# A two-layer decoder trunk handed its inputs in the layouts that its engines read: feature rows for the activations, 4 KB rows for the weights

## The chip, the cores and the metric

The kernel runs on one core of a Trainium2 chip, as one launch. The metric is device microseconds (us) of that launch; the median of three runs is taken. The work of the host ahead of the launch and behind it (which the change adds to) is not part of the metric.

## The reference

Two layers over 512 tokens with 2048 features, float32. Layer 0 is sparse attention: an indexer scores the causal keys, each query keeps 128 of them, and softmax attention with rotary positions runs over these. Layer 1 is stick-breaking attention over keys and values made from layer 0's output. Each layer ends alike:

```
y = (o * silu(g)) @ w_out                 # o: attention, g: gate path
x = layer_norm(4**0.25 * x + y, ln_g[i], ln_b[i])
x = x + (p[i] @ w_ple[i]) * sigmoid(x @ w_ple_gate[i])
```

The inputs are `x` (512 x 2048, tokens in rows), `p` (2 x 512 x 256), positions, the weights (each with the input features in rows) and the LayerNorm rows; the output has tokens in rows.

## The kernel before

All activations are kept with features on the 128 partitions and the 512 tokens along the free dimension, as tiles of 128 x 512 (`tt`, 78 buffers), 16 tiles to a full activation. float32 products are made of three matmuls (`mm3`): both operands are split into a high part, rounded by ScalarE, and the rest, taken by VectorE (`split` for activations, lines 103 and 104; `split_w` for weights, lines 314 and 315).

The kernel is one list of chunks, written out by hand in the order in which TensorE (PE) takes them. A chunk is 512 KB of weights (128 x 1024), loaded by `load` on SP's queue six chunks ahead into one of six `raw` buffers, split two chunks ahead, and used by 24 matmuls of 512 columns (lines 119 to 121). `run` emits them; small work (attention of a head, stores) is hung on the chunks by `after`, `mid`, `defer` and `soon`, and so takes its place in the order of each engine. Instructions of one engine run in the order of the program.

The stages, with their place in the span:

- start, 0 to 8 us: `prologue` loads x and the first weights, runs transposes on a constant to warm PE (`warm`), and turns and splits the first two x tiles.
- the value block, 8 to 58 us: `natural_block`, eight chunks. The weights are the moving operand; in the middle of each of seven chunks (`mid`) the next two x tiles are turned on PE by `transpose_x` (line 464) and split.
- the indexer, keys, queries and gates of layer 0 with the attention of its 16 heads, to 650 us. `ln_columns` (line 456) turns the LayerNorm rows there.
- `mix_out(0)`, `ple_chunks(0)`, `gate_block(0)`: output projection, embedding, LayerNorm and gate, to 1010 us. `prep_p` (line 778) turns the embeddings. `out_done` adds x back, from the high and the low part of its split (lines 802 and 803), which are therefore kept until then. Behind it come the sums of LayerNorm.
- layer 1's values, and from 1052 us on `quads`: keys, queries, values and gates by Strassen's scheme, with half-sized matmuls of 256 columns (line 198). Some chunks are sums of weight blocks: 60 of them come by a DMA that adds, issued by POOL (`add_load`, line 300), 60 by VectorE (line 305).
- `mix_out(1)`, `ple_chunks(1)`, `gate_block(1)`, from 1745 us to the end. `x1_load` (line 949) brings back layer 0's output, which was put into DRAM. `out_store` turns each output tile by four transposes (line 1117), copies it by ScalarE (line 1118) and stores it (line 1119); the last tile goes in two halves.

Weights lie in DRAM as the caller gives them, so a chunk is gathered in pieces of 512 B (128 columns), 1 KB (256) or 2 KB (512), in layer 0's query and gate blocks by two DMAs.

Of the kernel before, what the change touches and what calls it, by code (L numbers as in the profile page):

```python
# [74 lines left out]
class Kernel:  # L75
# [66 lines left out]
    def block(self, view, cols, xs, done, pops=1, col=0):  # L142
        outs = [Out(KT, lambda ps, i=i: done(i, ps), col) for i in range(2)]
        self.chunks += [self.chunk4(view, cols, kc, outs, xs, pops=pops) for kc in range(KT // 4)]
# [5 lines left out]
    def chunk4(self, view, cols, kc, outs, xs, pre=None, pops=1):  # L150
        nc = self.nc

        def loads(raw):
            r = raw.rearrange("p (k c) -> p k c", k=4)
            if view is None:
                cols(raw, kc)
            elif cols[1] == cols[0] + P:
                nc.sync.dma_start(r, view[:, 4 * kc:4 * kc + 4, cols[0]:cols[0] + 2 * P])
            else:
# [7 lines left out]
    def natural_block(self, view, col, xs, done):  # L167
        outs = [Out(KT, lambda ps, t=t: done(t, ps)) for t in range(NT)]
        for kc in range(KT // 2):
            def loads(raw, kc=kc):  # L170
                r = raw.rearrange("p (k c) -> p k c", k=2)
                for k in ((0, 1), (1, 2)) if kc == 0 else ((0, 2),):
                    self.nc.sync.dma_start(r[:, k[0]:k[1], :], view[:, 2 * kc + k[0]:2 * kc + k[1], col:col + T])
# [4 lines left out]
            ch = Chunk(loads, mms)  # L178
            ch.parts = 2 if kc == 0 else 1
            self.chunks.append(ch)  # L180

    def natural_halves(self, view, col, x, done):
        outs = [Out(KT, lambda ps, t=t: done(t, ps)) for t in range(NT)]
        for kc in range(KT // 2):
            def loads(raw, kc=kc):
                self.nc.sync.dma_start(raw.rearrange("p (k c) -> p k c", k=2),
                                       view[:, 2 * kc:2 * kc + 2, col:col + T])

            mms = [((k * T, 0), outs[t], (lambda m=2 * kc + k, t=t: x(m, t))) for t in range(NT) for k in range(2)]
            self.chunks.append(Chunk(loads, mms))  # L190
# [10 lines left out]
    def quads(self, sources, forms, done):  # L201
# [4 lines left out]
        def product(q, name, form, acc, start, stop, after, fresh=None, add=None, grown=None, plus=None):  # L206
# [7 lines left out]
            def rows(half, block):  # L214
                view, c = block
                return view[:, half::2, c:c + P]

            def loads(raw):
                nc.sync.dma_start(raw.rearrange("p (k c) -> p k c", k=8), rows(*fresh))

            ch = Chunk(loads if fresh else None, [])
# [74 lines left out]
    def add_load(self, c):  # L296
# [3 lines left out]
        self.nc.gpsimd.dma_start(ch.raw.rearrange("p (k c) -> p k c", k=8), ch.add, accum_op=OP.add)  # L300
# [88 lines left out]
def body(tc, x, p, positions, w_in_a, w_out_a, w_q_b, w_kv_b, w_out_b, ln_g, ln_b, w_ple, w_ple_gate, freq, out):  # L389
    nc = tc.nc  # L390
    with tc.tile_pool(name="const", bufs=1) as const, \
# [7 lines left out]
        _emit(k, x[0], p, positions, w_in_a[0], w_out_a[0], w_q_b[0], w_kv_b, w_out_b[0], ln_g, ln_b, w_ple,  # L399
              w_ple_gate, freq, out[0])  # L400


def _emit(k, x, p, positions, w_in, w_out_a, w_q, w_kv, w_out_b, ln_g, ln_b, w_ple, w_gate, freq, out):
    nc, const = k.nc, k.const
    kview = lambda w: w.rearrange("(k p) c -> p k c", p=P)
    win_v, wq_v, wkv_v = kview(w_in), kview(w_q), kview(w_kv)
    wout_v = [kview(w_out_a), kview(w_out_b)]
    wgate_v = [kview(w_gate[i]) for i in range(2)]
    wple_v = [kview(w_ple[i]) for i in range(2)]
# [8 lines left out]
    lnrow = const.tile([64, P], F32, name="lnrow")  # L418

    def load_small():  # L420
        nc.sync.dma_start(fr, freq)
        nc.sync.dma_start(pos_i, positions.to_broadcast([P, T]))
        nc.sync.dma_start(lnrow[0:32, :], ln_g.rearrange("i (m c) -> (i m) c", c=P))
        nc.sync.dma_start(lnrow[32:64, :], ln_b.rearrange("i (m c) -> (i m) c", c=P))

    xv = x.rearrange("(t p) d -> p t d", p=P)
# [21 lines left out]
    lncol = const.tile([P, 64], F32, name="lncol")  # L448
# [5 lines left out]
    def ln_columns():  # L454
        ps = k.ps("s")
        nc.tensor.transpose(ps[:, 0:64], lnrow, ident[0:64, 0:64])
        nc.vector.tensor_copy(lncol, ps[:, 0:64])

    def transpose_x(m):
        b, c = divmod(m, 2)  # L460
        ps = k.ps("s")
        for t in range(NT):
            off = (t % 2) * 2 * P + c * P
            nc.tensor.transpose(ps[:, t * P:(t + 1) * P], xin[b][t // 2][:, off:off + P], ident)  # L464
        xT[m] = k.split(ps)
        if c == 1:
            xin[b] = None
# [73 lines left out]
    def ki_block():  # L541
        o = Out(KT, lambda ps: ki_done(0, ps))
        for kc in range(2):
            def loads(raw, kc=kc):
                r = raw.rearrange("p (k c) -> p k c", k=8)
                nc.sync.dma_start(r[:, :, 0:64], win_v[:, 8 * kc:8 * kc + 8, KI0:KI0 + 64])
                nc.sync.dma_start(r[:, :, 64:128], win_v[:, 8 * kc:8 * kc + 8, WI0:WI0 + 64])

            mms = [(P * j, o, (lambda m=8 * kc + j: xT[m])) for j in range(8)]
            k.chunks.append(Chunk(loads, mms))  # L550
# [169 lines left out]
    def first_x(ms):  # L720
        for m in ms:
            transpose_x(m)

    k.natural_block(win_v, V0, xs, lambda t, ps: v_done(va, t, ps))
    for n in range(7):
        k.chunks[n].mid = lambda n=n: first_x(range(2 * n + 2, 2 * n + 4))
# [5 lines left out]
    def prologue():  # L732
        early = LOAD_LEAD - HL_BUFS + 1
        for n in range(early):
            load_x(n)
            k.ahead(n - LOAD_LEAD)
        for n in range(early, 8):
            load_x(n)
        load_small()
        warm(8)  # L740
        first_x(range(2))
        warm(8)
# [7 lines left out]
    for m in range(0, 8, 2):  # L750
        k.block(win_v, (I0 + m * P, I0 + (m + 1) * P), xs, lambda i, ps, m=m: qi_done(m + i, ps), col=P)
    k.chunks[16].after = lambda: st["later"].pop(0)()
    k.chunks[12].after = ln_columns
    for g in range(0, KV_A, 2):
        k.block(win_v, (K0 + g * P, K0 + (g + 1) * P), xs, lambda i, ps, g=g: k_done(g + i, ps))
    for h in range(HEADS):
        k.block(win_v, (Q0 + h * P, G0 + h * P), xs, lambda i, ps, h=h: q_done_a(h, i, ps))
# [6 lines left out]
    def load_p(layer):  # L764
        pb.clear()
        pv = p[layer][0].rearrange("(t p) d -> p t d", p=P)
        for t in range(0, NT, 2):
            pt = k.tt(s="pin")
            nc.sync.dma_start(pt.rearrange("p (t d) -> p t d", t=2), pv[:, t:t + 2, :])
            pb.append(pt)  # L770

    def prep_p(layer):
        pT[layer] = []
        for f in range(2):
            ps = k.ps("s")
            for t in range(NT):
# [381 lines left out]
```

## Time and profile before

| | |
|---|---|
| median of 3 runs | 2142.22 us (2141.61 to 2142.41) |
| the profiled execution | 2142.52 us |
| its span in the trace | 2140.6 us |
| matmul instructions (transposes among them) | 12305 |
| of these transposes of x, p, the output and the LayerNorm rows | 64, 16, 64, 1 |
| read from and written to DRAM | 234.65 MB, 12.06 MB |

The profile shows one execution. Engines are PE (matmul), PEld (its weight loads, which overlap), DVE (VectorE), ACT (ScalarE), POOL (GpSimd) and SP (which issues most DMAs). A duration is that of one instruction from start to end; matmuls overlap, so the distance of two starts is shorter than a duration. L119 is line 119 of the kernel.

### The profile page before, as it was taken

How to read it: one execution, taken by the hardware profiler on the slowest of the kernel's cores; microseconds unless marked ns; L12 is line 12 of the kernel's file. 1: busy time of each engine (PE TensorE's matmuls, PEld its weight loads, DVE VectorE, ACT ScalarE, POOL GpSimd, SP SyncE). 2: the span in 40 equal slices, each digit the busy share in tenths (PEclk: the TensorE clock that was granted, in tenths of full speed). 3: DMA queues.
4: the chain of work that ended last, by engine and by line, in shares of the span. 5: the costliest groups of instructions: out<-in, count | busy, mean ns of one | idle time of the engine just before them, and what ended most of it. 6: DMA issues, size and time to landing. Idle time of an engine off the chain costs nothing.

```text
span 2140.6 us, 31013 instructions
## 1 busy us (share of the span) xinstructions
PE 2120.4 (99%) x12305; PEld 1876.6 (88%) x12305; DVE 1354.5 (63%) x2065; ACT 967.8 (45%) x1530; POOL 262.1 (12%) x287
## 2 busy tenths in 40 slices
PE   9999999999999999999999999999999999999999
PEld 8987888888888887888899999999999988887887
DVE  4576976566566547635778777777777765447432
ACT  3564345455453226423555555445555453226422
POOL 5111000000000100000022122112222111010000
PEclk9999999999999999999999999999999999999999
DMA  7332332222222232433567777777867863332331
GB/s 222 109 89 80 106 90 79 70 79 69 79 89 92 93 101 79 131 115 121 116 135 133 150 141 138 149 148 146 160 124 146 167 200 109 118 118 78 100 120 57
DMA packets 368816, 248.72 MB, mean 116 GB/s; under 512 B 13664, under 2 KB 354720, under 8 KB 368672
## 3 DMA queue, kind: packets, MB, share of 16 engines
q1 hardware_dynamic: 306272, 215.29, 34.9%
q0 software_dynamic: 62400, 31.46, 11.9%
q8 instruction: 96, 1.57, 0.3%
q14 instruction: 48, 0.39, 0.1%
HBM read 234.65 MB, written 12.06 MB: 115 GB/s over the span
## 4 chain that ended last, share of the span: by engine, by line
PE 91%; DVE 4%; issue 3%; ACT 2%; POOL 1%; DMA 0%; SPq 0%; POOLq 0%; DVEq 0%; ACTq 0%
PE g L198 25%; PE g L119 19%; PE g L120 19%; PE g L121 19%; PE s L627 2%; PE o L120 1%; PE o L121 1%; PE o L119 1%; PE s L119 1%; DVE wl L315 1%; PE s L120 1%; PE s L121 1%; DVE z L888 1%; PE s L561 1%; DVE z L887 1%
## 5 line engine op out<-in xcount | busy, mean ns | idle before, releaser
L315 DVE TENSOR_TENSOR wl<-raw,wh 128x1024 fp32r<-128x1024 f32 (+1 forms) x453 | 555.6, 1231 | 388.0 <-ACT wh L314 384.3
L119 PE MATMUL g<-h,wh 128*128 128x512 f32 (+1 forms) x1808 | 704.6, 390 | 3.3 <-ACT h L103 3.3
L120 PE MATMUL g<-l,wh 128*128 128x512 f32 (+1 forms) x1808 | 698.8, 387 | 3.6 <-DVE l L104 3.6
L121 PE MATMUL g<-h,wl 128*128 128x512 f32 (+1 forms) x1808 | 698.6, 386 | 0.5 <-DVE wl L315 0.5
L314 ACT CAST wh<-raw 128x1024 fp32r<-128x1024 f32 (+1 forms) x453 | 473.2, 1049 | 330.9 <-PE g L120 216.3
L198 PE MATMUL g<-f,wh 128*128 128x256 f32 x3360 | 619.4, 284 | 0.0
L198 PEld LDWEIGHTS g<-f,wh 128*128 128x128 f32 x3360 | 528.6, 192 | 0.8
L198 PE MATMUL g<-f,wl 128*128 128x256 f32 x1680 | 475.5, 283 | 1.9 <-DVE wl L315 1.9
L119 PEld LDWEIGHTS g<-h,wh 128*128 128x128 f32 x1808 | 340.3, 188 | 74.4 <-ACT h L103 5.4
L120 PEld LDWEIGHTS g<-l,wh 128*128 128x128 f32 x1808 | 340.2, 188 | 70.3 <-DVE l L104 5.9
L121 PEld LDWEIGHTS g<-h,wl 128*128 128x128 f32 x1808 | 340.0, 188 | 67.0 <-DVE wl L315 1.0
L198 PEld LDWEIGHTS g<-f,wl 128*128 128x128 f32 x1680 | 322.0, 192 | 3.5 <-DVE wl L315 2.7
L300 POOL DMA_DIRECT2D raw<-in_w_q_b_dram x60 | 94.4, 1894 | 571.9 <-issue 244.1
L104 DVE TENSOR_TENSOR l<-s,h 128x512 fp32r<-128x512 f32 (+1 forms) x128 | 72.9, 617 | 45.7 <-ACT h L103 45.7
L504 POOL TENSOR_TENSOR rb<-rb,sin 128x512 f32<-128x512 f32 (+2 forms) x29 | 36.0, 1240 | 475.7 <-ACT rb L502 320.6
L685 ACT ACTIVATE pr<-pr,s 128x128 f32<-128x128 f32 (+1 forms) x64 | 36.0, 563 | 126.1 <-DVE s L684 125.7
L103 ACT CAST h<-s 128x512 fp32r<-128x512 f32 (+1 forms) x128 | 61.1, 540 | 59.9 <-PE s L464 31.0
L837 POOL TENSOR_TENSOR a<-a,sq 128x512 f32<-128x512 f32 x30 | 40.3, 1343 | 338.9 <-ACT sq L835 338.7
L305 DVE TENSOR_TENSOR raw<-raw,raw 128x1024 f32<-128x1024 f32 x60 | 73.1, 1218 | 0.0
L700 DVE TENSOR_TENSOR_SCAN r<-keep,zeros 128x127 f32<-128x127 f32 (+1 forms) x64 | 54.3, 849 | 13.7 <-POOL keep L697 13.7
L505 DVE TENSOR_TENSOR ra<-ra,cos 128x512 f32<-128x512 f32 (+2 forms) x29 | 32.8, 1130 | 37.7 <-ACT ra L503 37.6
L835 ACT ACTIVATE sq<-z 128x512 f32<-128x512 f32 x30 | 19.0, 634 | 81.7 <-DVE z L828 81.7
(187 smaller groups left out, 1960.3 us busy)
## 6 DMA issues: line engine op xcount, KB each, us to landing
raw<-in_w_in_a_dram SPq DMA_DIRECT2D x134, 256.0 KB, 3.3
raw<-in_w_ple_gate_dram SPq DMA_DIRECT2D x64, 512.0 KB, 3.8
raw<-in_w_kv_b_dram SPq DMA_DIRECT2D x64, 512.0 KB, 6.4
raw<-in_w_q_b_dram SPq DMA_DIRECT2D x64, 512.0 KB, 6.9
raw<-in_w_q_b_dram POOLq DMA_DIRECT2D x60, 512.0 KB, 10.0
raw<-in_w_out_a_dram SPq DMA_DIRECT2D x32, 512.0 KB, 3.6
raw<-in_w_out_b_dram SPq DMA_DIRECT2D x32, 512.0 KB, 3.5
raw<-in_w_in_a_dram SPq DMA_DIRECT2D x31, 512.0 KB, 3.8
```

What stands on the lines that cost most here:

```text
L103: nc.scalar.copy(h[:, lo:w], src[:, lo:w])
L104: nc.vector.tensor_tensor(l[:, lo:w], src[:, lo:w], h.bitcast(F32)[:, lo:w], op=OP.subtract)
L119: nc.tensor.matmul(out, ah, bh, start=start, stop=False)
L120: nc.tensor.matmul(out, ah, bl, start=False, stop=False)
L121: nc.tensor.matmul(out, al, bh, start=False, stop=stop)
L198: nc.tensor.matmul(ps[:, :HALF], a, b, start=start and j == 0 and n == 0, stop=stop and j == KT // 2 - 1 and n == 2, skip_group_check=True)
L300: self.nc.gpsimd.dma_start(ch.raw.rearrange("p (k c) -> p k c", k=8), ch.add, accum_op=OP.add)
L305: self.nc.vector.tensor_tensor(ch.raw, ch.raw, ch.plus.raw, op=OP.add)
L314: nc.scalar.copy(ch.h[:, i:i + w], ch.raw[:, i:i + w])
L315: nc.vector.tensor_tensor(ch.l[:, i:i + w], ch.raw[:, i:i + w], ch.h.bitcast(F32)[:, i:i + w], op=OP.subtract)
L627: nc.tensor.transpose(banks[b][:, off + (i - j) * P:off + (i - j + 1) * P], a["p"][i][:, j * P:(j + 1) * P], ident)
L700: nc.vector.tensor_tensor_scan(r[:, 0:n - 1][:, ::-1], keep[:, 1:n][:, ::-1], zeros.to_broadcast([P, n - 1]), 1.0, op0=OP.mult, op1=OP.add)
```

## The change

The host hands over other arrays, and the kernel drops what turned them:

- `x`, `p` and the output have features in rows, the LayerNorm rows come as columns (128 x 64). `transpose_x`, `ln_columns` and the transposes of `prep_p` and `out_store` go, as does the copy in `out_store`. A tile of x or p is loaded in pieces of 2 KB and split from SBUF instead of PSUM.
- every weight chunk lies in DRAM as 128 rows of 4 KB, in the order of use; one DMA loads it (`whole`). Columns of the value weights of layer 1's first heads are held twice (`w_v` and `w_kv`).
- in the start, the order of the loads is x tile 0, half of the first weight chunk, x tile 1, the other half; the warm-up's 16 transposes stand in one group.
- layer 0's output projection loads x again (16 tiles on SP's queue) instead of keeping its split; the split is given up at the end of the last head. `out_done` has one addition.
- an output store is hung on the next chunk by `soon` instead of `defer_by`.

```
-    def chunk4(self, view, cols, kc, outs, xs, pre=None, pops=1):
-        def loads(raw):
-            r = raw.rearrange("p (k c) -> p k c", k=4)
...
-                for i in range(2):
-                    nc.sync.dma_start(r[:, :, i * P:(i + 1) * P], view[:, 4 * kc:4 * kc + 4, cols[i]:cols[i] + P])
+    def whole(self, src, n):
+        return lambda raw: self.nc.sync.dma_start(raw, src[n])
+    def chunk4(self, src, n, kc, outs, xs, pre=None, pops=1):
...
-        return Chunk(loads, mms, pre=pre, pops=pops)
+        return Chunk(self.whole(src, n), mms, pre=pre, pops=pops)
...
-        self.nc.gpsimd.dma_start(ch.raw.rearrange("p (k c) -> p k c", k=8), ch.add, accum_op=OP.add)
+        self.nc.gpsimd.dma_start(ch.raw, ch.add, accum_op=OP.add)
...
-    def load_x(b):
-        xin[b] = [k.tt(s="xin") for _ in range(2)]
-        for t in range(2):
-            nc.sync.dma_start(xin[b][t].rearrange("p (t c) -> p t c", t=2),
-                              xv[:, 2 * t:2 * t + 2, b * 2 * P:(b + 1) * 2 * P])
+    def load_x(m):
+        xin[m] = k.tt(s="xin")
+        nc.sync.dma_start(xin[m], xt[m])
...
-    def transpose_x(m):
-        b, c = divmod(m, 2)
-        ps = k.ps("s")
-        for t in range(NT):
-            off = (t % 2) * 2 * P + c * P
-            nc.tensor.transpose(ps[:, t * P:(t + 1) * P], xin[b][t // 2][:, off:off + P], ident)
-        xT[m] = k.split(ps)
+    def split_x(m):
+        xT[m] = k.split(xin.pop(m))
...
+    def first_loads(raw):
+        for i in range(2):
+            if i:
+                load_x(1)
+            nc.sync.dma_start(raw[:, i * T:(i + 1) * T], w_in[0][:, i * T:(i + 1) * T])
...
+    for kc in range(4):
+        k.chunks[kc - 4].then(lambda kc=kc: x_drop(kc))
...
     def prep_p(layer):
-        for f in range(2):
-            ps = k.ps("s")
-            for t in range(NT):
-                off = (t % 2) * 256 + f * P
-                nc.tensor.transpose(ps[:, t * P:(t + 1) * P], pb[t // 2][:, off:off + P], ident)
-            pT[layer].append(k.split(ps))
+        pT[layer] = [k.split(t) for t in pb]
...
-            nc.vector.scalar_tensor_tensor(z, xh.bitcast(F32), ALPHA, ps, op0=OP.mult, op1=OP.add)
-            nc.vector.scalar_tensor_tensor(z, xl.bitcast(F32), ALPHA, z, op0=OP.mult, op1=OP.add)
+        nc.vector.scalar_tensor_tensor(z, x1.pop(m), ALPHA, ps, op0=OP.mult, op1=OP.add)
...
-            if layer == 1 and kc == 1:
+            if kc == 1:
+                ch.then(lambda b=b: [x1_load(layer, 2 * b + i) for i in range(2)])
+    def x1_load(layer, m):
         x1[m] = k.tt(s="x1")
-        nc.sync.dma_start(x1[m], xd[m])
+        nc.sync.dma_start(x1[m], xd[m] if layer else xt[m])
...
     def out_store(m, v):
-        o = k.tt(s="out")
         for c in halves(m):
...
-                nc.tensor.transpose(ps[:, t * P:(t + 1) * P], v[:, t * P:(t + 1) * P], ident)
-            nc.scalar.copy(o[:, c], ps[:, c])
-            nc.sync.dma_start(outv[:, t0:t1, m * P:(m + 1) * P], o[:, c].rearrange("p (t c) -> p t c", t=t1 - t0))
+            nc.sync.dma_start(out[m, :, c], v[:, c])
```

## Rows read from the trace of the kernel before

**Rows 1.** The page, busy time, share and instructions of each engine.

```profile
PE 2120.4 (99%) x12305; PEld 1876.6 (88%) x12305; DVE 1354.5 (63%) x2065; ACT 967.8 (45%) x1530; POOL 262.1 (12%) x287
```

**Rows 2.** Stretches: length, busy PE, PEld, DVE, ACT, POOL, granted clock, DMA share, GB/s.

```profile
0.00:5.00 5.00, 2.67 (x11) 1.87 (x11) 0.23 (x2) 1.28 (x1) 1.28 (x9) 1.00 0.58 168
...
12.00:20.00 8.00, 8.00 (x45) 6.80 (x44) 3.63 (x5) 2.92 (x5) 0.00 (x0) 1.00 1.09 357
20.00:56.00 36.00, 36.00 (x180) 30.23 (x179) 16.19 (x19) 12.89 (x19) 31.36 (x23) 1.00 0.59 163
...
800.00:870.00 70.00, 66.31 (x282) 52.25 (x281) 55.96 (x78) 43.40 (x64) 2.59 (x2) 1.00 0.24 76
...
1095.00:1240.00 145.00, 143.10 (x1161) 141.29 (x1160) 110.67 (x152) 75.99 (x124) 30.96 (x45) 1.00 0.72 139
1240.00:1735.00 495.00, 495.00 (x4059) 492.08 (x4058) 362.63 (x473) 251.53 (x402) 102.03 (x128) 1.00 0.78 153
...
1770.00:1920.00 150.00, 150.00 (x667) 124.24 (x666) 69.33 (x76) 42.38 (x51) 17.58 (x13) 1.00 0.36 116
...
1920.00:1990.00 70.00, 66.76 (x281) 53.36 (x280) 55.52 (x77) 44.16 (x64) 2.58 (x2) 0.98 0.23 75
```

**Rows 3.** Order of time, PE, one chunk of the value block: start, length.

```profile
43.56 0.39 PE L121 MATMUL g<-wh,l 128*128 128x512 f32 x1
...
44.90 0.40 PE L120 MATMUL g<-wl,h 128*128 128x512 f32 x1
...
49.90 0.39 PE L121 MATMUL g<-wh,l 128*128 128x512 f32 x1
```

**Rows 4.** Groups by line, two kinds of transposes: busy us, mean ns.

```profile
L1117 PE MATMUL s<-ident,sg 128*128 128x128 f32 x64 | 9.8, 273 | 1.4 <-DVE sg L961 1.4
...
L456 PE MATMUL s<-ident,lnrow 64*128 64x64 f32 x1 | 0.3, 271 | 0.0
```

**Rows 5.** Order of time, the first 14 us.

```profile
4.99 1.54 PE L464 MATMUL s<-ident,xin 128*128 128x128 f32 x6 [0.75 <-DMA xin<-in_x_dram]
...
6.57 0.59 ACT L103 CAST h<-s 128x512 fp32r<-128x512 f32 x1 [0.27 <-PE s L464]
...
7.89 0.77 PE L119 MATMUL g<-wh,h 128*128 128x512 f32 x1
...
13.37 1.29 DVE L104 TENSOR_TENSOR l<-s,h 128x512 fp32r<-128x512 f32 x2 [0.54 <-ACT h L103]
```

**Rows 6.** The chain that ended last, its first 20 us: start, length.

```profile
10.17 0.43 PE g L120
...
10.91 0.23 PE g L119
...
12.28 0.87 PE s L464 x8
18.62 0.87 PE s L464 x8
```

**Rows 7.** Order of time, ScalarE's sigmoid of the gate blocks, both layers.

```profile
984.85 0.60 ACT L959 ACTIVATE sg<-g 128x512 f32<-128x512 f32 x1 [1.89 <-PE g L121]
...
1006.61 0.60 ACT L959 ACTIVATE sg<-g 128x512 f32<-128x512 f32 x1 [1.89 <-PE g L121]
...
2063.59 0.60 ACT L959 ACTIVATE sg<-g 128x512 f32<-128x512 f32 x1 [1.20 <-PE g L121]
...
2086.30 0.60 ACT L959 ACTIVATE sg<-g 128x512 f32<-128x512 f32 x1 [1.20 <-PE g L121]
```

**Rows 8.** The chain that ended last, its last pieces.

```profile
2136.12 0.43 DVE sg L961
...
2137.14 0.37 ACT out L1118
```

**Rows 9.** DMA issues (KB each, us to landing), and ScalarE's waits from 1240 us.

```profile
raw<-in_w_q_b_dram POOLq DMA_DIRECT2D x60, 512.0 KB, 10.0
...
ACT wh L314 <- DMA raw<-in_w_q_b_dram: 4.2, 5, 2.6
```

More of the change, by code (lines that the diff above doesn't have):

```diff
@@ L140, in pop, with block @@
                 n -= 1
-    def block(self, view, cols, xs, done, pops=1, col=0):
+    def block(self, src, base, xs, done, pops=1, col=0):
         outs = [Out(KT, lambda ps, i=i: done(i, ps), col) for i in range(2)]
-        self.chunks += [self.chunk4(view, cols, kc, outs, xs, pops=pops) for kc in range(KT // 4)]
+        self.chunks += [self.chunk4(src, base + kc, kc, outs, xs, pops=pops) for kc in range(KT // 4)]
     def zip_last(self):
@@ L214, in rows @@
             def rows(half, block):
[L215 to L221, printed above, removed]
+                src, n = block
+                return src[2 * n + half]
+            ch = Chunk((lambda raw: nc.sync.dma_start(raw, rows(*fresh))) if fresh else None, [])
             ch.product = run
@@ L417, in _emit @@
     pos_i = k.t.tile([P, T], I32, tag="t", name="pos_i")
-    lnrow = const.tile([64, P], F32, name="lnrow")
+    lncol = const.tile([P, 64], F32, name="lncol")
     def load_small():
@@ L447, in _emit @@
     pos = k.tt(s="pos")
-    lncol = const.tile([P, 64], F32, name="lncol")
     def prepare():
@@ L718, in q_done_a @@
         slots(a, h, soft_tile)
[L720 to L724, printed above, removed]
+    k.natural_block(w_in, xs, lambda t, ps: v_done(va, t, ps))
+    first = k.chunks[0]
+    first.parts = 2
+    def first_loads(raw):
[3 more added lines that the diff above has]
+            nc.sync.dma_start(raw[:, i * T:(i + 1) * T], w_in[0][:, i * T:(i + 1) * T])
+    first.loads = first_loads
     for n in range(7):
-        k.chunks[n].mid = lambda n=n: first_x(range(2 * n + 2, 2 * n + 4))
+        k.chunks[n].mid = lambda n=n: (split_x(2 * n + 2), split_x(2 * n + 3))
     def warm(n):
@@ L733, in prologue @@
         early = LOAD_LEAD - HL_BUFS + 1
[L734 to L738, printed above, removed]
+        load_x(0)
+        k.ahead(-LOAD_LEAD)
+        for n in range(1, 8):
+            load_x(2 * n)
+            load_x(2 * n + 1)
+            if n < early:
+                k.ahead(n - LOAD_LEAD)
         load_small()
-        warm(8)
-        first_x(range(2))
-        warm(8)
+        warm(16)
+        split_x(0)
+        split_x(1)
         for n in range(early - LOAD_LEAD, 0):
@@ L1140, in _freq, with _pairs, _natural, _parity @@
     return f
-def kernel(**inputs):
+def _pairs(w, pairs):
+    v = w.reshape(4, 4, P, -1)
+    v = np.stack([np.concatenate([v[..., a:a + P], v[..., b:b + P]], -1) for a, b in pairs])
+    return v.transpose(0, 1, 3, 2, 4).reshape(-1, P, 1024)
+def _natural(w, width):
+    return w.reshape(-1, 2, P, width // T, T).transpose(3, 0, 2, 1, 4).reshape(-1, P, 1024)
+def _parity(w):
+    return w.reshape(8, 2, P, -1, P).transpose(3, 1, 2, 0, 4).reshape(-1, P, 1024)
+def _w_in(w):
+    col = lambda c: w[:, c:c + 64]
+    ki = np.concatenate([col(KI0), col(WI0)], -1).reshape(2, 8, P, P).transpose(0, 2, 1, 3).reshape(2, P, 1024)
+    blocks = [(c + m * P, c + (m + 1) * P) for c, n in ((I0, 8), (K0, KV_A)) for m in range(0, n, 2)]
+    blocks += [(Q0 + h * P, G0 + h * P) for h in range(HEADS)]
+    return np.concatenate([_natural(w[:, V0:V0 + T], T), ki, _pairs(w, blocks)])
@@ L1144 @@
+def kernel(x, p, positions, w_in_a, w_out_a, w_q_b, w_kv_b, w_out_b, ln_g, ln_b, w_ple, w_ple_gate):
     import concourse.bacc as bacc
     from concourse.bass_utils import run_bass_kernel_spmd as run
+    blocks = [(c, c + P) for c in range(0, D, 2 * P)]
+    arrays = dict(
+        x=np.asarray(x)[0].T.reshape(KT, P, T),
+        p=np.asarray(p)[:, 0].transpose(0, 2, 1).reshape(2, 2, P, T),
+        positions=np.asarray(positions),
+        ln=np.concatenate([np.asarray(ln_g).reshape(32, P), np.asarray(ln_b).reshape(32, P)]).T,
+        freq=_freq(),
+        w_in=_w_in(np.asarray(w_in_a)[0]),
+        w_out=np.stack([_pairs(np.asarray(w)[0], blocks) for w in (w_out_a, w_out_b)]),
+        w_gate=np.stack([_pairs(w, blocks) for w in np.asarray(w_ple_gate)]),
+        w_ple=np.stack([_natural(w, D) for w in np.asarray(w_ple)]),
+        w_kv=_parity(np.asarray(w_kv_b)),
+        w_v=_natural(np.asarray(w_kv_b)[:, D:D + T], T),
+        w_q=_parity(np.asarray(w_q_b)[0]),
+    )
```

110 lines of the change are left out of this document (30 added, 80 removed).

## The prediction

> **What bounds the kernel now.** I read the shares of the engines first. TensorE (PE) is busy 2120.4 us of a span of 2140.6 us, every other engine at most 63% [rows 1]. Then the table by stretch. The reader should look at PE's column beside DMA's: the stage of the 256-column products has PE busy 495.00 of 495 us while the DMA engines are at 0.78, and layer 1's output projection has 150.00 of 150 [rows 2]. So PE doesn't wait for a load in the long stages, whatever the DMA engines do. Of the 20.2 us in which PE is idle, 2.3 lie in the first 5 us, 3.7 and 3.2 in the two LayerNorm stretches [rows 2]; the rest is mostly at the end and behind stage changes. What PE does not execute is therefore nearly a pure gain, and what the DMA engines do better is hidden until it reaches one of the idle places.
>
> Busy time alone misleads about a price, because matmuls overlap. I take prices from start times: two matmuls with 512 columns start 0.227 us apart, and a group of transposes costs what it stretches this distance by.
>
> **Part 1, x handed over in feature rows.** 64 transposes go: 16 tiles, four each. From the matmul at 43.56 to the second one behind a group of eight, at 44.90, pass 1.34 us [rows 3]; two steps of 0.227 are 0.454, so eight cost 0.885 us. The pitch says the same: from 43.56 to 49.90, a chunk later, pass 6.34 us, and 24 x 0.227 is 5.45. Seven groups lie inside the first block: 7 x 0.885 = 6.2 us. The eighth is in the start, below. The pair of casts that splits a tile stays, and reads SBUF instead of PSUM; in this block ScalarE and VectorE are below half busy [rows 2], so I price that at nothing; if that cover were gone, it would cost these casts' own extra time.
>
> The rows also give one transpose of the output a duration of 273 ns in the mean [rows 4], and whoever multiplies all 145 by it gets 40 us. By the start times eight cost 0.885 us, 0.11 each, since they overlap. I take these; the 40 us become a rival. The Trainium skill, TensorE: Matmul & The Clock Gate, Part 4, gives about 275 ns for a 128x128 transpose inside a kernel; the trace agrees with it as a duration, and as a price it would make the sum that of the rival.
>
> **Start.** Before, the second xin transfer landed at 4.99, then came transposes, the second x cast at 6.57 and the first matmul at 7.89 [rows 5]: 1.32 us from that cast to the matmul. Now the cast waits for no transposes, but for x tile 1, which is third in the queue (behind x tile 0 and half of the first weight chunk), each 256 KB. At 357 GB/s [rows 2] 256 KB take 0.73 us, so I put it at 4.99 + 0.73 = 5.72 and the matmul at 7.05: 0.8 us earlier. Upper bound: landing as early as the second, 4.99, gives 1.6. For the lower bound, the clock. The first matmuls here are 0.43 us apart, the 1.2 GHz level; the chain has a step of 0.43 at 10.17 and one of 0.23 at 10.91 [rows 6]. (The column of the granted clock reads 1.00 from the start [rows 2]; the steps show the level.) Some six matmuls ran at the lower level; the warm-up is now 16 transposes in one go, with a pause behind them until the first matmul. I take six again; if it is twelve, that is 6 x 0.2 = 1.2 us and the start is worth -0.4.
>
> The Trainium skill, DMA: Bandwidth & Descriptors, Specifications, sets an HBM limit of about 358 GB/s a core beside a fabric ceiling of 435. By the first, larger pieces land no sooner than these 1 KB ones and the sum stays; by the second my estimate is that three of 256 KB land some 0.4 us sooner, and the sum grows by as much. The trace's 357 at a share above 1 speaks for the first.
>
> **Part 2, LayerNorm columns.** One transpose of 64 columns: between an eighth of a group (0.11) and its own duration, 0.27 [rows 4]; I take 0.2.
>
> **Part 3, p in feature rows.** 16 transposes, two tiles of four in each layer's output projection, so one group of eight a layer: 2 x 0.885 = 1.8 us. Their splits stay.
>
> **Part 4, output in feature rows.** 64 transposes and 17 copies on ScalarE go. A block of the gate takes 1006.61 - 984.85 = 21.76 us in layer 0, which stores without transposes, and 2086.30 - 2063.59 = 22.71 in layer 1 [rows 7]. The difference, 0.95, is two groups of four: 0.475 a group. 14 of the 16 groups lie between matmuls: 6.65 us. The one of tile 14 runs beside the last sigmoid. Tile 15 is on the path of the end: from the start of its last sum on VectorE (2136.12, 0.43 long, done 2136.55) to the end of the copy at 2137.51 [rows 8] pass 0.96 us, and the store is now issued behind that sum: 1.0 us. Landing in pieces of 1 KB instead of 512 B is worth 0 to 0.3, I take 0.
>
> **Part 5, x read again in layer 0's output projection.** New: 16 loads of 256 KB on SP's queue, two behind the second chunk of each block, in place of keeping the split x. One of two VectorE additions a tile goes. Queued behind such a load on SP are the weight loads; they run six chunks ahead, 6 x 5.45 = 33 us. Layer 1 already does exactly this with 16 loads, and its stretch has PE at 150.00 of 150 [rows 2], so the loads cost nothing; without that cover a pair costs its transfer, 1.5 us, 12 us for eight. The shorter VectorE chain can only help the LayerNorm behind it: layer 0 leaves PE idle 3.69 us there, layer 1, with the single addition, 3.24 [rows 2]. Bounds 0 and 0.45; I take 0.2.
>
> **Part 6, weights as rows of 4 KB.** Every weight load becomes one DMA with 128 pieces where there were up to 1024 and in part two DMAs. It shortens the DMA share and SP's and POOL's issues. All of it lies under a PE that is not waiting, so 0. A gain isn't excluded where PE waits behind ScalarE or VectorE, but these waits aren't for loads; the nearest are the 1.9 us at the start of the 256-column stage (143.10 of 145 [rows 2]), so bounds 0 and 1.9.
>
> **Sum.** 6.2 + 0.8 + 0.2 + 1.8 + 6.65 + 1.0 + 0.2 = 16.85 us. The profiled execution took 2142.52 us (span 2140.6), giving 2125.7; the median of the runs, 2142.22, is 0.3 lower: 2125.4. I forecast 2125.5.
>
> **Rivals.**
> (a) The first block becomes bound by its supply. Without transposes chunk 1 would begin at 7.05 + 6 x 0.43 + 18 x 0.227 = 13.7 and needs x tile 3's low half at its sixth matmul, 14.8. Before, VectorE finished that half at 14.66 [rows 5]; behind no transposes it can't be later, unless its cast waits for the weights ahead of it in ScalarE's order. It is a near miss of tenths. From there a chunk needs 1 MB in 5.45 us, 2.9 at the rate above. If the rate halved (5.9 us), six chunks would lose 0.45 each; with the boundary 3 us in all: 2128.5. With the slow clock of the start added, 2130. Chance 0.10.
> (b) Slower: the accumulating loads. 60 loads with addition on POOL's queue land after 10.0 us in median [rows 9]; five times in their stage ScalarE's cast waited for one, 2.6 us at worst, with PE unharmed [rows 2, 9]. The split runs two chunks ahead of PE; a chunk is 24 x 0.122 = 2.9 us (495 us / 4059 matmuls [rows 2]), so the cover is at most 5.8. If adding in pieces of 4 KB instead of 512 B made a landing longer than 15.8 us, each of the 30 pairs of such loads would pass the surplus on: from 0.6 us of surplus (16.4 us) the gain is gone, and at 17.8 us the loss is 2 x 30 = 60 less 17, 2185. Against it: fewer pieces, same bytes, lower DMA share. Chance 0.03.
> (c) The new x loads stop SP until a buffer comes free, and weights come late. That would need a stop beyond 33 us; the buffers of the split x are now given up earlier, so I see none. Gain half or wholly lost, 2134 to 2142. Chance 0.03.
> (d) More than counted: transposes cost their durations (40 us, 2102), or matmuls stand closer when the DMA engines rest. The second speaks for itself if spacing followed DMA: but 12.28 to 18.62 is 6.34 us at a share of 1.09 [rows 2, 6], and 43.56 to 49.90 is 6.34 at 0.59 [rows 2, 3]. Chance of such a thing 0.04.
>
> **How the numbers follow.** The sum holds with 0.80. Its own bounds: less 1.2 (clock) and 0.2 (LayerNorm) is 2127, more 0.8, 0.25, 0.3 and 1.9 is 2122.3, all at once. Taking (a) in up to 2130 gives a range of 2122.5 to 2130. A difference under 0.2%, 4.3 us, is what a measurement of this kernel can't tell from none. Faster by more: 0.80 + 0.10 + 0.04 = 0.94; the same 0.03 (c); slower 0.03 (b).
>
> **What would show it.** In the profile after: no matmul on ident with xin, pin, lnrow or sg; a pitch of 5.45 us in the first block; gate blocks of 21.76 us in layer 1; first matmul near 7.05 and full speed some 2.6 us later; PE idle near 3.2 us in layer 0's LayerNorm; the last store behind the last sum. The DMA share of the 256-column stage falls well below 0.78 with PE still full. Wrong it would be by new waits of PE: for l, h or wl in the first 20 us (a), for wl behind POOL's loads (b), for z in layer 0's output (c).

## The result and the profile after

The kernel with the change takes 2125.24 us in the median (five runs, 2123.66 to 2125.29), the kernel before beside it 2142.22 (2141.61 to 2145.38). The ratio is 0.9915, 95% interval 0.9904 to 0.9926: 17 us faster. The profiled execution took 2125.29 us, its span is 2123.6: 17.06 us less than the 2140.6 of before.

The page's first part (answers to [rows 1]):

```profile
PE 2102.4 (99%) x12160; PEld 1861.1 (88%) x12160; DVE 1343.6 (63%) x2048; ACT 958.6 (45%) x1513; POOL 221.8 (10%) x287
```

145 matmul instructions are gone and PE is busy 18.0 us less, so the span shrank by nearly what PE no longer executes.

The table by stretch (columns as in [rows 2]; the stretches lie where the same work now stands, the last is the end of the 256-column stage):

```profile
12.00:20.00 8.00, 8.00 (x37) 6.64 (x36) 6.03 (x8) 4.18 (x6) 0.00 (x0) 1.00 1.06 387
20.00:56.00 36.00, 36.00 (x161) 29.80 (x160) 19.68 (x20) 14.11 (x19) 33.13 (x22) 1.00 0.47 176
800.00:870.00 70.00, 66.81 (x281) 53.41 (x280) 55.30 (x79) 46.25 (x70) 1.29 (x1) 0.98 0.23 80
1240.00:1715.00 475.00, 475.00 (x3896) 472.21 (x3895) 348.25 (x453) 240.16 (x381) 68.37 (x121) 1.00 0.55 149
1755.00:1900.00 145.00, 145.00 (x641) 120.04 (x640) 67.64 (x74) 41.41 (x50) 17.57 (x13) 1.00 0.35 121
1735.00:1755.00 20.00, 18.20 (x78) 15.09 (x79) 13.52 (x20) 10.87 (x18) 0.00 (x0) 0.91 0.46 160
```

PE is still full in the long stretches. The DMA share of the 256-column stage fell from 0.78 to 0.55 and PE has nothing of it there: 475.00 of 475, as before 495.00 of 495.

One chunk of the value block, in order of time on PE (answers to [rows 3]): its first matmul and that of the next chunk.

```profile
44.80 0.39 PE L119 MATMUL g<-wh,h 128*128 128x512 f32 x1
...
50.24 0.39 PE L119 MATMUL g<-wh,h 128*128 128x512 f32 x1
```

5.44 us where 6.34 passed before. The same distance in layer 1's gate, between sigmoids of ScalarE (answers to [rows 7]):

```profile
2050.81 0.60 ACT L905 ACTIVATE sg<-g 128x512 f32<-128x512 f32 x1 [1.89 <-PE g L121]
...
2072.57 0.60 ACT L905 ACTIVATE sg<-g 128x512 f32<-128x512 f32 x1 [1.89 <-PE g L121]
```

21.76 us, what layer 0 always took, for 22.71. The start, in order of time (answers to [rows 5]), and the chain that ended last in the same stretch (to [rows 6]):

```profile
6.23 0.62 ACT L103 CAST h<-xin 128x512 fp32r<-128x512 f32 x1 [2.05 <-DMA xin<-in_x_dram]
...
7.42 0.62 PE L119 MATMUL g<-wh,h 128*128 128x512 f32 x1 [2.68 <-ACT wh L291]
```

```profile
1.70 4.50 DMA xin<-in_x_dram
...
9.02 0.43 PE g L121
...
10.73 0.43 PE g L119
...
11.41 0.23 PE g L121
```

x tile 1 arrives at 6.2 us, the first matmul starts 0.47 us earlier than before, and the matmuls up to 11.15 stand 0.43 us apart, the level of 1.2 GHz. Before, that ended at 10.9 [rows 6]. So nothing is won by the twelfth matmul.

Without the warm-up and the turned x, p, output and LayerNorm rows, the same 12144 matmuls are in both traces, in the same order. The difference of their starts, read behind each part, tells what each part was worth:

| part | predicted, us | measured, us |
|---|---|---|
| start, to the twelfth matmul | 0.8 | -0.05 |
| x, seven groups | 6.2 | 6.26 |
| LayerNorm columns | 0.2 | 0.41 |
| p, two groups | 1.8 | 0.89 + 0.90 |
| LayerNorm of layer 0 | 0.2 | -0.18 |
| from there to the end of the 256-column stage | 0 | -0.13 |
| end of the 256-column stage | 0 | 0.73 |
| LayerNorm of layer 1 | 0 | 0.14 |
| output, 14 groups | 6.65 | 6.67 |
| from the last matmul to the end | 1.0 | 1.42 |
| sum | 16.85 | 17.06 |

### The profile page after: what moved, and what is told of

Its sections match the earlier page's. It is cut to its first block, busy times and chain, and to the rows that moved or that the text cites. A ratio compares the mean times of both kernels' runs of the same rounds, so it can differ in the third digit from the quotient of the medians.

```text
span 2123.6 us, 30583 instructions
## 1 busy us (share of the span) xinstructions
PE 2102.4 (99%) x12160; PEld 1861.1 (88%) x12160; DVE 1343.6 (63%) x2048; ACT 958.6 (45%) x1513; POOL 221.8 (10%) x287
## 4 chain that ended last, share of the span: by engine, by line
PE 89%; DVE 4%; issue 4%; ACT 2%; POOL 1%; DMA 0%; SPq 0%; POOLq 0%; DVEq 0%; ACTq 0%
PE g L178 24%; PE g L119 19%; PE g L120 19%; PE g L121 19%; PE s L576 2%; PE o L120 1%; PE o L121 1%; PE o L119 1%; DVE wl L292 1%; PE s L119 1%; DVE z L838 1%; PE s L120 1%; PE s L121 1%; PE s L510 1%; DVE z L837 1%
## 5 line engine op out<-in xcount | busy, mean ns | idle before, releaser
L277 POOL DMA_DIRECT2D raw<-in_w_q_dram x60 | 53.0, 1038 | 591.3 <-issue 279.5
L104 DVE TENSOR_TENSOR l<-s,h 128x512 fp32r<-128x512 f32 (+1 forms) x108 | 59.9, 604 | 18.5 <-ACT h L103 18.5
L103 ACT CAST h<-s 128x512 fp32r<-128x512 f32 (+1 forms) x108 | 50.2, 531 | 25.9 <-PE s L1003 13.4
L642 ACT ACTIVATE keep<-s 128x128 f32<-128x128 f32 (+1 forms) x64 | 28.1, 439 | 55.5 <-PE s L121 55.5
```

The lines of the kernel that those rows point to most:

```text
L103: nc.scalar.copy(h[:, lo:w], src[:, lo:w])
L104: nc.vector.tensor_tensor(l[:, lo:w], src[:, lo:w], h.bitcast(F32)[:, lo:w], op=OP.subtract)
L277: self.nc.gpsimd.dma_start(ch.raw, ch.add, accum_op=OP.add)
```

## The experiments

The question was no longer the total but its odd terms: why the start gave nothing, what the larger pieces of the weights did after all, and whether a group of transposes costs PE time or something around it.

### The weights as rows of 4 KB, alone, and everything else, alone

The first kernel is that of before with the weights of the change; the second that of the change with the weights of before.

```
     def chunk4(...)                                   # e1_rows: before, with
-        return Chunk(loads, mms, pre=pre, pops=pops)
+        return Chunk(self.whole(src, n), mms, pre=pre, pops=pops)
...
-        self.nc.gpsimd.dma_start(ch.raw.rearrange("p (k c) -> p k c", k=8), ch.add, accum_op=OP.add)
+        self.nc.gpsimd.dma_start(ch.raw, ch.add, accum_op=OP.add)
     # e2_turns: the change, with the same lines the other way round
```

> The kernel before with the weights alone handed over as rows of 4 KB; all transposes stay. Theory (the gain is what TensorE no longer executes, and larger pieces reach the end only where TensorE waits): 2141 to 2142.5 us; the value block keeps its pitch of 6.34 us, layer 1's gate blocks stay at 22.71 us, the DMA share of the 256-column stage falls from 0.78 to about 0.55, and the one wait that shrinks is that at the end of that stage, from 3.5 to about 2.5 us. Rival (the larger pieces carry a good part of the 17 us, since all stages move faster with less DMA traffic): 2133 to 2138 us.

> The changed kernel with the weights left in the caller's layout (pieces of 512 B to 2 KB); x, p, output and LayerNorm columns as changed. Theory: 2125 to 2127 us, that is nearly the whole gain, with the wait at the end of the 256-column stage back at about 3.5 us and the DMA share there back near 0.78. Rival (larger pieces carry part of it): 2129 to 2134 us.

Measured: the weights alone 2140.72 us beside 2142.93 of before, ratio 0.999 (0.9981 to 0.9999). The rest alone 2125.89, ratio 0.9923 (0.991 to 0.9935). So the 17 us come without the new weights, and the new weights are worth something between 0.2 and 4.1 us, a little more than I expected. The steps are as expected: with the weights alone the value block has a pitch of 6.37 us, a gate block of layer 1 takes 22.71 us, and the DMA share of the 256-column stage is 0.57; with the rest alone it is 0.77. The traces say where the rest of the difference lies. PE's waits at the end of the 256-column stage, for VectorE's low halves, total, times, longest: first before, then the weights alone, then the rest alone.

```profile
PE s L627 <- DVE l L104: 3.5, 1, 3.5
```

```profile
PE s L593 <- DVE l L104: 2.5, 1, 2.5
```

```profile
PE s L609 <- DVE l L104: 3.6, 1, 3.6
```

The kernel of the change has 2.5 there as well. One pause of PE is 1 us shorter with the new weights, with or without the rest of the change. (The trace of the weights alone flatters them: behind that pause its clock did not fall, where that of the kernel before did, which is 1.4 us more. The last section tells how irregular that is.) Further back on the path stands a cast of ScalarE that splits a chunk. In order of time on ScalarE: before, the rest alone, and the change.

```profile
1729.77 1.05 ACT L314 CAST wh<-raw 128x1024 fp32r<-128x1024 f32 x1 [2.56 <-DMA raw<-in_w_q_b_dram]
```

```profile
1723.65 1.05 ACT L314 CAST wh<-raw 128x1024 fp32r<-128x1024 f32 x1 [2.71 <-DMA raw<-in_w_q_dram]
```

```profile
1719.90 1.05 ACT L291 CAST wh<-raw 128x1024 fp32r<-128x1024 f32 x1
```

With the old pieces that cast waits 2.6 to 2.7 us for the last of the 60 accumulating loads. VectorE takes the low half of the same chunk behind it, and so starts late; before:

```profile
1730.85 1.23 DVE L315 TENSOR_TENSOR wl<-raw,wh 128x1024 fp32r<-128x1024 f32 x1 [3.67 <-ACT wh L314]
```

From there VectorE works without a pause up to 1741.80, the end of the halves that PE waits for. In the change it pauses three times on the same way, 1.3 us in all, for PE and POOL. So of the 2.6 us about 1 us reaches PE. The kernels also differ in SP's loads, though, so the next experiment parts the two.

### The accumulating loads alone as rows of 4 KB

```
-        self.nc.gpsimd.dma_start(ch.raw.rearrange("p (k c) -> p k c", k=8), ch.add, accum_op=OP.add)   # on e2_turns
+        self.nc.gpsimd.dma_start(ch.raw, ch.add, accum_op=OP.add)
```

> The changed kernel with the weights in the caller's layout as in e2_turns, but the 60 loads that add read rows of 4 KB. In e2_turns PE waited 3.6 us at the end of the 256-column stage, in the changed kernel 2.5. My theory (the last load that adds came late there): these loads land after 6 to 8 us instead of 10, ScalarE's cast of the last one waits for nothing, PE waits 2.4 to 2.7 us there. Rival (all weight traffic in small pieces slows the end of the stage): PE waits 3.3 us or more, although these loads have large pieces.

Measured: one run, 2124.2 us. Its DMA issues (KB each, us to landing), its cast on ScalarE and PE's wait:

```profile
raw<-in_w_q_dram POOLq DMA_DIRECT2D x60, 512.0 KB, 6.7
```

```profile
1720.02 1.05 ACT L314 CAST wh<-raw 128x1024 fp32r<-128x1024 f32 x1
```

```profile
PE s L610 <- DVE l L104: 2.5, 1, 2.5
```

The loads land after 6.7 us instead of 10.0 [rows 9], the cast waits for nothing, and the pause is 2.5 us, although SP's loads still have their small pieces. The theory holds: the 1 us is that of the accumulating loads, and the wait on this path is for the last of them.

The 1.42 us of the end part the same way. From the start of the last matmul to the end of the span pass 6.61 us before, 6.28 with the weights alone, 5.57 and 5.59 in the two kernels with the rest and SP's old weights, 5.19 to 5.21 in every kernel with all of the change. So 1.02 to 1.09 us go with the output, as predicted, and 0.33 to 0.40 with the weights on SP's queue, although no weight is loaded any more there.

What the weights change is SP's place in a round. Each DMA of SP's queue tells its landing by one of eight semaphores, which are taken in turn, and behind the last store SP waits for all eight in a fixed order, 0.06 us for each. SP's waits from the landing of the last store on, before and in the change, that of the store itself included:

```profile
L1154 SPq EVENT_SEMAPHORE  x7: 27/28/28, 2139.4 to 2139.7; - x7
```

```profile
L1128 SPq EVENT_SEMAPHORE  x2: 28/28/28, 2122.6 to 2122.7; - x2
```

Before, SP issues 530 DMAs and the last store stands second in the order, so six waits are left behind it. The change issues 479 and has one left, the weights alone 464 and none, the two kernels with SP's old weights 545 and seven. From the landing to the end of the span pass 1.26, 0.96, 0.91, and 1.32 and 1.33 us; the other eight traces have one wait left and 0.96 or 0.97. So the length of the rows has no part in it: five waits fewer are 0.30 us of the 1.42. The landing of the last store itself, 1.85 us behind the last computing instruction before and 1.71 in the change with its larger pieces, is 0.14 more. The other 0.98 are the transposes and the copy, as e6_out_turned shows below. (The pairs above give 1.02 to 1.09 for the last two together, since in each pair the kernel without the transposes has one wait more.)

### The price of a group of transposes

```
-        k.chunks[n].mid = lambda n=n: (split_x(2 * n + 2), split_x(2 * n + 3))
+        k.chunks[n].mid = lambda n=n: (warm(8), split_x(2 * n + 2), split_x(2 * n + 3))
```

> The changed kernel with eight transposes of the constant put into the middle of each of seven chunks of the value block; nothing reads them, and no cast waits for them. My theory (the price of a group is PE's own execution, 0.885 us): the distance of chunks in the block goes from 5.44 back to 6.33 us, and the time rises by 6.2 to about 2131.4. First rival (the price came from handing the turned tile over in PSUM to ScalarE and VectorE): the distance stays under 5.8 us, the time under 2128. Second rival (a transpose costs its duration of 0.27 us): 15 us, 2140.

Measured: one run, 2132.12 us. PE in order of time, around two groups:

```profile
44.25 0.40 PE L121 MATMUL g<-wh,l 128*128 128x512 f32 x1
44.48 1.04 PE L686 MATMUL o<-ident 128*128 128x128 f32 x8
45.28 0.48 PE L119 MATMUL g<-wh,h 128*128 128x512 f32 x1
45.59 0.40 PE L120 MATMUL g<-wl,h 128*128 128x512 f32 x1
...
50.82 1.04 PE L686 MATMUL o<-ident 128*128 128x128 f32 x8
```

From 44.25 to 45.59 pass 1.34 us, less two steps of 0.227 that is 0.886: the price of [rows 3] as closely as the rows can tell, by transposes that nobody reads. The pitch is 6.34 again. The price is PE's own. The time rose by 6.8: by the starts of the same matmuls six groups cost 0.90 each, the first, still in part at 1.2 GHz, 1.1, and the start 0.4, longer at 1.2 GHz; 0.1 came back in later stages. The Trainium skill (TensorE: Matmul & The Clock Gate, Part 4) gives about 275 ns for a transpose of 128x128, measured with bf16; the trace agrees with it as a duration (273 in [rows 4]), but eight of them cost 0.89 us and not 2.2.

### The output turned again

The change with the transposes and the copy of its output put back; each 128 x 128 block of its output stands turned.

```
-        k.soon(lambda: out_store(m, v))
+        k.defer_by(1, lambda: out_store(m, v))
...
+            for t in range(c.start // P, c.stop // P):
+                nc.tensor.transpose(ps[:, t * P:(t + 1) * P], v[:, t * P:(t + 1) * P], ident)
+            nc.scalar.copy(o[:, c], ps[:, c])
+            nc.sync.dma_start(out[m, :, c], o[:, c])
```

> The changed kernel with the output's transposes and ScalarE's copy put back and the store hung one chunk later as before; the 128 x 128 blocks are stored turned in place, so each piece of a store has its old size of 2 KB or 1 KB, and the output's blocks are turned. My theory (14 groups inside the block at 0.475 us, and the path behind the last matmul): a gate block of layer 1 takes 22.7 us again instead of 21.76, from the start of the last matmul to the end of the span pass 6.4 to 6.6 us instead of 5.19, and the time is 2133 (2132 to 2134). Rival (what was won there came from the smaller pieces of the store): the last stretch stays under 5.6 us. Second rival (transposes cost their durations of 0.27 us): 2142.

Measured: one run, 2131.07 us. Sigmoids of ScalarE a block apart, and its last instruction:

```profile
2052.49 0.60 ACT L905 ACTIVATE sg<-g 128x512 f32<-128x512 f32 x1 [1.24 <-PE g L121]
...
2075.20 0.60 ACT L905 ACTIVATE sg<-g 128x512 f32<-128x512 f32 x1 [1.24 <-PE g L121]
...
2126.04 0.37 ACT L1061 COPY out<-s 128x256 f32<-128x256 f32 x1 [0.42 <-PE s L1060]
```

A block takes 22.71 us again. The end takes 6.17 us, 0.98 more than in the change and less than the 6.4 to 6.6 that I wrote: the 1.0 us of the prediction is all that transposes and copy cost there. The total missed my 2132 to 2134 because this execution lost less elsewhere: x tile 1 was cast at 5.19 and the first matmul started at 6.38, and PE kept 2.4 GHz at the end of the 256-column stage. A total of one run doesn't tell 2 us here; the distances inside the trace do.

### x read again

```
-        nc.vector.scalar_tensor_tensor(z, x1.pop(m), ALPHA, ps, op0=OP.mult, op1=OP.add)
+        if m in x1:
+            nc.vector.scalar_tensor_tensor(z, x1.pop(m), ALPHA, ps, op0=OP.mult, op1=OP.add)
+        else:
+            xh, xl = xT[m]
+            nc.vector.scalar_tensor_tensor(z, xh.bitcast(F32), ALPHA, ps, op0=OP.mult, op1=OP.add)
+            nc.vector.scalar_tensor_tensor(z, xl.bitcast(F32), ALPHA, z, op0=OP.mult, op1=OP.add)
...
-            if kc == 1:
+            if kc == 1 and layer == 1:
```

> The changed kernel, with layer 0's output projection as before: the split x is kept and added in two steps, and x isn't loaded again. My theory (the loads are hidden and the shorter chain on VectorE only touches the LayerNorm pause): the same time within 0.7 us of 2125.2; PE's idle time in the LayerNorm stretch of layer 0 goes back from 3.2 to about 3.7 us. Rival (loading x again delays weights or costs PE time): 3 us or more faster than 2125.2.

Measured: one run, 2125.3 us, span 2123.6, the change's own. The LayerNorm stretch, columns as above:

```profile
800.00:870.00 70.00, 66.77 (x281) 53.42 (x281) 56.68 (x81) 46.28 (x70) 1.29 (x1) 0.98 0.24 80
```

The loads cost nothing, as predicted. But PE's idle time stayed at 3.23 us; my theory wanted 3.7. The single addition doesn't shorten the stretch either. The idle time had shrunk for another reason: in the change and here the granted clock of the stretch is 0.98, PE runs some matmuls at 1.2 GHz behind its pause, and so is longer busy. Between the same two matmuls around the stretch pass 39.68 us before, 39.86 in the change, and 39.70 to 39.76 in the three kernels that add x once and in which nothing ran at 1.2 GHz there, e7_dummy, e3_bridge and e8_bridges (the last two below). In these three PE is idle for 3.65 to 3.71 us between those matmuls, like the kernel before with its 3.69; in the nine traces whose clock fell there, for 3.19 to 3.26, whether x is added once or twice.

### The start

Two kernels: more transposes in the warm-up, so that PE's pause before the first matmul shrinks; and x tile 1 ahead of all weights.

```
     # e3_bridge
-        warm(16)
+        warm(28)
     # e4_x1_first
-            if i:
-                load_x(1)
...
         load_x(0)
+        load_x(1)
```

> The changed kernel with 28 warm-up transposes instead of 16, so that TensorE is busy from 1.4 us up to its first matmul near 7.4. Theory of the start (the pause of 2.7 us ahead of the first matmul is why eight matmuls, not six, ran at the lower level): the first matmul stays near 7.4 us, six or fewer run 0.43 us apart, and the 13th matmul starts 0.4 us or more earlier than the changed kernel's 12.16. Rival (what the transposes do is of no account, or the level comes at a set time): eight as before and 12.16 again, later if the longer group runs past 7.4 us. Time 2124 to 2126 either way.

> The changed kernel with x tile 1 loaded ahead of the first half of the weights instead of behind it. Theory (the first matmul waits behind x tile 1's cast, which is ahead of the weights' cast in ScalarE's order): the cast of x tile 1 begins near 5 us instead of 6.23, the weights' cast near 6.2 instead of 6.75, and the first matmul starts near 6.9 instead of 7.42. Rival (the first half of the weights then lands last and nothing is won): first matmul at 7.3 to 7.6. Time 2124 to 2126 either way.

Measured, one run each: 2122.91 and 2123.91 us. The first 14 us by the table of stretches, the change and then the longer warm-up; and PE there in order of time:

```profile
0.00:14.00 14.00, 9.71 (x37) 7.94 (x38) 5.86 (x10) 7.34 (x11) 1.27 (x9) 0.88 0.85 307
```

```profile
0.00:14.00 14.00, 11.99 (x59) 10.28 (x60) 6.15 (x10) 7.64 (x11) 1.28 (x9) 1.00 0.88 314
```

```profile
6.40 0.50 PE L119 MATMUL g<-wh,h 128*128 128x512 f32 x1 [0.28 <-ACT wh L291]
...
7.55 0.40 PE L121 MATMUL g<-wh,l 128*128 128x512 f32 x1
7.78 0.40 PE L119 MATMUL g<-wh,h 128*128 128x512 f32 x1
...
9.83 0.39 PE L119 MATMUL g<-wh,h 128*128 128x512 f32 x1
```

The granted clock is 1.00 instead of 0.88, and the thirteenth matmul starts 3.43 us after the first instead of 4.74. The first one stands at 6.40 and not near 7.4, because x tile 1 was cast at 5.21 in this execution; so the time is 1.1 us under the range that I wrote, and only 1.31 of the 2.33 us by which the thirteenth is earlier go with the warm-up. The trace of e6_out_turned, with the warm-up of the change and its first matmul at the same place, shows the difference alone:

```profile
1.42 3.68 PE L686 MATMUL o<-ident 128*128 128x128 f32 x16 [1.42 <-POOL ident L384]
6.38 0.80 PE L119 MATMUL g<-wh,h 128*128 128x512 f32 x1 [1.29 <-ACT wh L291]
```

There the thirteenth starts 4.96 us after the first. The transposes show the level too: they start 0.21 us apart at 1.2 GHz and 0.11 apart at 2.4. In e3_bridge the step changes at 4.4 us, within the warm-up. In e6_out_turned all 16 stand 0.21 apart and the first matmuls 0.43 apart, so its clock had not risen at all (the granted clock reads 1.00 there as in the kernel before; the steps show the level). In the change it had risen for the last three transposes, and fell again behind the pause of 2.68 us. So 28 transposes do two things: they last until the clock is up, and they leave no long pause behind. With x tile 1 first nothing is won, as its rival said; ScalarE and PE in order of time:

```profile
3.44 1.34 ACT L103 CAST h<-xin 128x512 fp32r<-128x512 f32 x2 [1.37 <-DMA xin<-in_x_dram]
6.61 1.27 ACT L291 CAST wh<-raw 128x512 fp32r<-128x512 f32 x2 [1.83 <-DMA raw<-in_w_in_dram]
7.28 0.50 PE L119 MATMUL g<-wh,h 128*128 128x512 f32 x1 [2.19 <-ACT wh L291]
```

On ScalarE the cast of x tile 1 stands ahead of that of the weights, so in either order three transfers of 256 KB lie ahead of the first matmul, and the third is late. How late differs between executions of the same loads: x tile 1 is cast at 5.19, 5.21, 5.79, 5.84, 5.91, 6.18, 6.19 and 6.23 us in the eight traces with the loads of the change.

### Both pauses of PE filled, twice

The longer warm-up, and 20 transposes of the constant ahead of the last two turned tiles at the end of the 256-column stage. As the clock differs between executions, this kernel was run again beside the change.

```
+                if j == 2 and "bridge" in a:
+                    warm(20)
...
-        warm(16)
+        warm(28)
...
+        if h == HEADS - 1:
+            a["bridge"] = True
```

> The changed kernel with two of PE's pauses filled by transposes of the constant: 28 instead of 16 in the warm-up, and 20 ahead of the last two turned tiles at the end of the 256-column stage. My theory (PE falls to 1.2 GHz behind a pause, and the matmuls 0.43 us apart are the price): the first 13 matmuls without one 0.43 us apart, no fall of the granted clock in the 30 us behind the stage's end, 2121.5 to 2123.5 against 2125.2. Rival (the clock falls whatever PE did in the pause, or the transposes come too early or late and cost what they win): 2124.5 to 2127.

> The changed kernel once more, unaltered, on the chip of the next run. My theory (the fall of the clock behind a pause, and the landing of x tile 1, differ from execution to execution): 2123.5 to 2126; its trace may show other falls than the first one, and the steps between the pauses (5.44 us a chunk, 21.76 us a gate block) to 0.02 us the same.

> The kernel of e8_bridges once more, unaltered, beside the changed kernel. My theory: 2121.5 to 2123, 1.5 to 4 us under the changed kernel on the same chip, no matmuls 0.43 us apart in the start and at the end of the 256-column stage. Rival (what e8_bridges won was its chip's): both kernels within 1 us of each other.

Measured: 2122.11 us (2121.86 to 2122.47, ratio to before 0.99, 0.9884 to 0.9917); on another chip 2122.10 (2121.39 to 2122.55, 0.9907, 0.9894 to 0.9921) beside the change at 2124.31 (2123.77 to 2124.99, 0.9919, 0.9905 to 0.9932). So filling the pauses is worth 2.2 us on that chip, by the medians; this is the fastest version. In its first trace, PE in order of time at the end of the stage, and its stretches there:

```profile
1732.31 2.35 PE L688 MATMUL o<-ident 128*128 128x128 f32 x20
1734.99 0.44 PE L578 MATMUL s<-ident,beta 128*128 128x128 f32 x2 [0.33 <-DVE l L104]
```

```profile
1735.00:1755.00 20.00, 20.00 (x93) 16.68 (x94) 12.95 (x19) 10.18 (x16) 0.00 (x0) 1.00 0.56 195
```

VectorE still sets when the last two tiles are turned; but the clock stays at 1.00 where the change had 0.91. The second trace of the change, at the same place and in the start, answers how regular that fall is:

```profile
0.00:14.00 14.00, 10.05 (x37) 8.33 (x38) 6.29 (x10) 7.74 (x11) 1.28 (x9) 0.88 0.86 311
...
1735.00:1755.00 20.00, 18.25 (x85) 15.20 (x86) 13.38 (x20) 10.77 (x18) 0.00 (x0) 1.00 0.57 185
```

The start lost its clock again, the stage's end didn't. There the bridge won nothing in the second comparison, and what it won came from the start, whose thirteenth matmul is 3.44 us behind the first with the bridge and 5.01 without. The two traces are 1.3 us apart; the rest of the 2.2 lies in executions that were not traced.

## Why the prediction was right, and where its steps were not

The total, 2125.5, came within 0.3 us, but not every step did. **Parts 1, 3 and 4** held: 6.26 for 6.2, 0.89 and 0.90 for 0.885 each, 6.67 for 6.65. Read from start times, the price of a group carried over to about 0.01 us, and e7_dummy shows that it is PE's execution and nothing in the hand-over to ScalarE.

**Start** was mis-sized: 0.8 foreseen, -0.05 measured. Both of its halves were out. The landing was put at 5.72; in this execution it was 6.2, within what the runs of the same loads show (5.19 to 6.23). And behind a warm-up in one go about eight matmuls ran at 1.2 GHz, between my six and the twelve of the lower bound; e3_bridge shows that the warm-up decides it. My six came from a kernel whose clock had not yet risen when its matmuls began: before, its 16 transposes on the constant also stand 0.21 apart to the last. The change's clock was up, and fell.

**Part 2** was mis-sized: 0.41 for 0.2, beyond both my bounds. A lone transpose between matmuls of 384 columns costs more than an eighth of a group and more than its own duration of 0.27; no run here takes that apart.

**Part 5** was right on the loads and wrong on the gain. That the LayerNorm's idle time falls was argued from two idle times, 3.69 and 3.24, of two stretches. The lower one had a granted clock of 0.98 [rows 2], which I passed over: slower matmuls had filled idle time. So the sign "idle near 3.2 us" came true, 3.19, for a reason that I had not seen, and the stretch grew by 0.18. e5_keep_x shows that the second addition costs nothing.

**Part 6** failed as an argument though the value lay inside its bounds. It said that the places where PE waits behind ScalarE or VectorE don't wait for loads. One did, two steps back: PE for VectorE, which stood behind ScalarE's cast, which waited for an accumulating load; [rows 9] shows such a wait of ScalarE, 2.6 us at worst, and I took it as covered. e1_rows, e2_turns and e9_adds show the 1 us. In the sum only 0.73 of it is left, as the change lost more clock behind its shorter pause than the kernel before behind its longer one.

**The end** was right for what it priced, 0.98 for 1.0; larger pieces of the store gave 0.14 of the 0 to 0.3 that I took at nothing. The other 0.30 I had not foreseen: five of SP's closing waits, which follow from the number of its DMAs.

In the table, two misses downwards (start -0.85, LayerNorm of layer 0 -0.38) met three upwards (stage end 0.73, end 0.42, columns 0.21). The range had room for that, but the closeness of the total is in part luck.

The rivals: **(a)** did not happen; the block is full from 12 us on (8.00 of 8, 36.00 of 36) at a pitch of 5.44. The rate there rose to 387 GB/s where I had counted with 357. Of the two figures that I cited from the Trainium skill, 358 is thus no limit for this core; its page Perfetto Trace Analysis, section Roofline, says that a core alone can exceed it up to its DMA engines, about 435, and the 387 agrees. x tile 1 landed no sooner for it. **(b)** went the other way, 10.0 to 6.2 us. This is the change's row of DMA issues:

```profile
raw<-in_w_q_dram POOLq DMA_DIRECT2D x60, 512.0 KB, 6.2
```

**(c)** is refuted by e5_keep_x. **(d)** is refuted by e7_dummy; and the DMA share of the 256-column stage fell from 0.78 to 0.55 with the matmuls as close as before (475 us for 3896, 495 for 4059: 0.122 each).

## What to carry to other kernels

On an engine that is always busy, the price of work is by how much it pushes the start of the next instruction, not its duration; taken so, it adds up. Where an engine's long wait is named for its neighbour, follow the neighbour's own waits back until one is for nothing or for a DMA, before an edit to the loads is priced at zero. A warm-up has to last until the step of its own transposes falls, and up to the first matmul. A pause of TensorE can cost twice, once as idle time and once in slower matmuls behind it; compare the distance of the same two instructions in both traces, since idle time alone goes down when the clock does.

## What was not expected of the hardware

The fall to 1.2 GHz behind a pause is not the same in every execution. At the end of the 256-column stage, behind a pause of 2.5 us, it came in four of nine traces and cost 1.4 to 1.6 us there (20.2 to 20.3 for 18.7 to 18.8 us between the same two matmuls); behind 3.5 us in both; with the pause filled in neither of two. In the start matmuls ran at 1.2 GHz in all eight traces with the change's 16 transposes in one go: the thirteenth stands 4.64 to 5.67 us behind the first (e7_dummy left out, with its group in between), against 3.43 to 3.44 in the three traces with 28. But only in four of the eight (the change twice, e4_x1_first, e9_adds) had the clock been up before, so that it fell; in the other four the transposes stood 0.21 us apart to the last and the matmuls were slow from the first. When the clock first rises differs as well: with 28 transposes their step changes at 4.4, 4.8 and 6.6 us, the last time with four of them left. In the LayerNorm of layer 0 the fall came in nine of thirteen traces and cost only 0.1 to 0.25 us.

The landing of three first loads of 256 KB varied by 1 us. And the close of a kernel, behind the landing of its last store, took 0.91 to 1.33 us, by 0.06 us for each of SP's eight closing waits that was still left.
